# One set of 4 KB slots for all stages, and w_out's hi/lo parts kept in DRAM, in a retention and conv-FFN block

## The chip, the cores and the metric

The kernel runs on one core of a Trainium2 chip. The metric is the device time of one execution in microseconds (us). It is the median of several runs, and lower is better.

## The reference

One encoder layer on `x` of 2048 tokens by 1024 channels, in float32:

```python
proj = x @ w_in                                  # 1024 x 2560 -> q | k | v | g | p
ret  = retention(rope(q), rope(k) * 128**-0.5, v)   # 4 heads of 128, chunks of 64, state carried on
ret  = rmsnorm_head(ret) * silu(g)
pool = (trailing_mean(p, windows 2,4,8,16) - p) @ w_pool * pool_scale    # per group of 128
x = layernorm(alpha * x + concat(ret, pool) @ w_out)       # 1024 x 1024
val, gate = split(x @ w_up)                      # 1024 x 5632
x = layernorm(alpha * x + (silu(causal_conv3(gate)) * val) @ w_down)     # 2816 x 1024
```

## The kernel before, in words

**Arithmetic.** Each float32 operand of a large product is cut into a rounded part and its remainder (`split`, L87: a cast on ACT, L88, and a subtraction on DVE, L89). `mm3` (L91 to L94) makes a product from three matmuls: hi x hi, hi x lo, lo x hi. So an operand tile of 128 x 512 takes 4 KB of each partition for its two parts.

**Seven products for eight.** The three large multiplications work on 2 x 2 blocks by a seven-product scheme (`PRODUCTS`, L47): each pair of weight tiles (i) has seven products p1, p6, p2, p5, p7, p3, p4, whose left operands (`OPERANDS`: a11, s2, s1, a12, s3, a22, s4) are blocks of the activations or sums of blocks, and whose right ones (b.. and t..) are blocks of the weights or sums of them. One superblock is 1024 tokens; there are two. `class Seven` (L181) holds the operands of one superblock in seven tiles of 16 KB (a product each, four parts j), loads the weights four products ahead (`LOOK`, L53), makes the weights' sums in the first superblock and stores them to DRAM on POOL's queue (`w_sums`), and reads them back in the second (`again`, L249).

**Four stages.** `stage_in` (L518) makes q, k, v, p, g, in 10 pairs per superblock, and stores them to `proj`. The first pair is done in the plain way (`first_pair`, L259), with the sums of x made after it (`first_sums`, L206). During pairs 2 to 5 the sums of the second superblock are made and stored (`sums_to_dram`, L172), at pair 6 the first pair's weight sums, and at pairs 4 to 8 `fold` (L555) multiplies the pool group's matrix into the matching half of w_out and stores it to `w_pool_out`. In the second superblock the steps of retention and pooling (`Light`, L342) are laid between the products, 1.7 per product. `stage_mix` (L612) loads w_out (half of it from `w_pool_out`), splits it into `wo` tiles (L619 to L624), and for each of four blocks of 512 tokens multiplies (`contract`, L637), adds x, does the layer norm, and turns the rows (`turn`, L645: 8 transposes on PE, 2 copies on ACT, DMAs to `x1T` and `y1`). `stage_up` (L713) has 22 pairs per superblock, and makes and stores the gated, convolved activations and their sums (`to_down`, L750). `stage_down` (L810) multiplies by w_down and does the last norm.

**Memory.** Each stage opens pools of its own and closes them at its end; a later pool's tile that lies over an earlier one's waits for the last use of that tile. Shared by all stages are a ring of six 4 KB tiles for split weights (`new_w`, L146) and twelve 2 KB temporaries, five of them for loads of activations (`new_x`, L152) and seven for raw weights (`new_raw`, L153).

**Order.** The program is written as one stream; a scheduler at build time lays each engine's and each DMA queue's instructions out by its own estimate of when they are ready, the earlier in the program first among those that are. It may bring an instruction far forward. Instructions made through `behind` (L106) keep their order. At run time every queue goes in its order. Loads are issued on SP's queue, stores on POOL's.

## Time and profile before

| What | us |
|---|---|
| Median of 3 runs | 2059.79 (2059.72 to 2061.27) |
| The profiled execution, its own time | 2060.84 |
| Its span, first to last instruction | 2059.1 |
| TensorE busy in the span | 1960.2 |
| VectorE busy | 1418.5 |
| ScalarE busy | 807.4 |
| GpSimd busy | 406.8 |

The stages lie in the span at about 0 to 500 us (`stage_in`, its second superblock from 250), 500 to 755 (`stage_mix`), 755 to 1620 (`stage_up`, its second superblock from 1200) and 1620 to 2059 (`stage_down`). Where TensorE is fed, a product's matmuls start one after another; a stretch in which it was idle, or ran at the lower clock, shows as fewer matmuls than its length allows. The memory traffic over the whole span is 433.98 MB.

### The profile page before, as it was taken

The numbers are of one execution on the slowest core, as the hardware profiler recorded it, in microseconds if no ns is written. First come the engines' busy times: TensorE is split into PE (matmuls) and PEld (weight loads), VectorE is DVE, ScalarE is ACT, GpSimd is POOL, SyncE is SP. The second block draws the span as 40 slices with busy tenths as digits, with TensorE's granted clock in tenths as the row PEclk, the third lists the DMA queues.
The fourth block names the chain that finished last, engine by engine and source line by source line (L and its number), as shares of the span: only waits on it lengthen the run. The fifth ranks groups of instructions, "written<-read, shape, count | busy, mean of one in ns | idle before, by whom it ended". The sixth has DMA issues, their size and how long they took to land.

```text
span 2059.1 us, 26395 instructions
## 1 busy us (share of the span) xinstructions
PE 1960.2 (95%) x8849; PEld 1610.5 (78%) x8849; DVE 1418.5 (69%) x2167; ACT 807.4 (39%) x1314; POOL 406.8 (20%) x692
## 2 busy tenths in 40 slices
PE   7998899997899969989999999999999899999997
PEld 5777788886778847878888878888888688888886
DVE  6655687766675668778778786777766654455687
ACT  5334634433332235434444454444444443333321
POOL 1332112221132332233223211222211000000022
PEclk9999999999899989999999999999999999999999
DMA  8886788887777586575444574877744684444443
GB/s 270 281 270 238 231 245 233 242 266 247 232 229 226 205 276 218 184 235 192 157 158 170 169 258 131 280 252 242 268 144 154 224 312 143 140 136 128 156 166 124
DMA packets 195496, 433.98 MB, mean 211 GB/s; under 512 B 26272, under 2 KB 26272, under 8 KB 195360
## 3 DMA queue, kind: packets, MB, share of 16 engines
q1 hardware_dynamic: 148672, 278.64, 43.9%
q0 software_dynamic: 46112, 152.60, 20.3%
q8 instruction: 69, 1.13, 0.2%
q10 hardware_dynamic: 576, 1.05, 0.1%
q14 instruction: 67, 0.55, 0.1%
HBM read 277.53 MB, written 154.66 MB: 210 GB/s over the span
## 4 chain that ended last, share of the span: by engine, by line
PE 77%; DMA 8%; issue 7%; DVE 5%; POOL 2%; ACT 1%; SPq 0%; POOLq 0%; DVEq 0%; ACTq 0%
PE psz L94 9%; PE psz L92 9%; PE psz L93 9%; PE psy L93 7%; PE psy L92 7%; PE psy L94 7%; PE psw L92 6%; PE psw L93 6%; PE psw L94 6%; PE pl L104 3%; PE pl L93 2%; PE pl L94 2%; PE pl L92 2%; DMA mr<-mixT 1%; DMA xq<-in_xT 1%
## 5 line engine op out<-in xcount | busy, mean ns | idle before, releaser
L92 PE MATMUL psy<-opa,w 128*128 128x512 f32 x516 | 207.0, 401 | 16.0 <-ACT opa L88 12.2
L92 PE MATMUL psz<-ops,w 128*128 128x512 f32 x508 | 202.5, 399 | 9.2 <-ACT keptp L722 5.5
L93 PE MATMUL psy<-opa,w 128*128 128x512 f32 x516 | 205.1, 398 | 0.0
L94 PE MATMUL psy<-opa,w 128*128 128x512 f32 x516 | 204.2, 396 | 0.0
L94 PE MATMUL psw<-ops,w 128*128 128x512 f32 x504 | 198.1, 393 | 5.0 <-DVE w L89 5.0
L92 PE MATMUL psw<-ops,w 128*128 128x512 f32 x504 | 199.9, 397 | 1.8 <-ACT ops L88 0.9
L94 PE MATMUL psz<-ops,w 128*128 128x512 f32 x508 | 200.6, 395 | 0.0
L93 PE MATMUL psz<-ops,w 128*128 128x512 f32 x508 | 200.5, 395 | 0.1
L93 PE MATMUL psw<-ops,w 128*128 128x512 f32 x504 | 198.1, 393 | 0.7 <-DVE ops L89 0.7
L92 PEld LDWEIGHTS psy<-opa,w 128*128 128x128 f32 x516 | 99.3, 192 | 38.6 <-ACT opa L88 13.4
L92 PEld LDWEIGHTS psz<-ops,w 128*128 128x128 f32 x508 | 96.4, 190 | 32.9 <-ACT keptp L722 7.2
L313 POOL TENSOR_TENSOR rs<-mv,neg_half 128x1 f32<-128x1 f32 x32 | 38.4, 1200 | 410.4 <-DVE mv L329 410.1
L93 PEld LDWEIGHTS psy<-opa,w 128*128 128x128 f32 x516 | 99.0, 192 | 22.6 <-DVE opa L89 1.7
L94 PEld LDWEIGHTS psw<-ops,w 128*128 128x128 f32 x504 | 95.1, 189 | 26.0 <-DVE w L89 5.4
L94 PEld LDWEIGHTS psy<-opa,w 128*128 128x128 f32 x516 | 98.6, 191 | 21.3
L92 PEld LDWEIGHTS psw<-ops,w 128*128 128x128 f32 x504 | 95.3, 189 | 23.4 <-ACT ops L88 1.8
L94 PEld LDWEIGHTS psz<-ops,w 128*128 128x128 f32 x508 | 96.5, 190 | 21.0
L93 PEld LDWEIGHTS psz<-ops,w 128*128 128x128 f32 x508 | 96.3, 190 | 21.0 <-DVE ops L89 1.1
L93 PEld LDWEIGHTS psw<-ops,w 128*128 128x128 f32 x504 | 95.3, 189 | 21.1 <-DVE ops L89 1.2
L92 PE MATMUL psz<-opa,w 128*128 128x512 f32 x256 | 100.7, 393 | 0.0
L94 PE MATMUL psz<-opa,w 128*128 128x512 f32 x256 | 100.1, 391 | 0.0
L93 PE MATMUL psz<-opa,w 128*128 128x512 f32 x256 | 100.1, 391 | 0.0
(372 smaller groups left out, 4705.7 us busy)
## 6 DMA issues: line engine op xcount, KB each, us to landing
u_ops<-us POOLq DMA_DIRECT2D x88, 256.0 KB, 3.2
proj<-o POOLq DMA_DIRECT2D x80, 256.0 KB, 4.5
u_ops<-zz POOLq DMA_DIRECT2D x66, 256.0 KB, 2.6
again<-w_sums_in SPq DMA_DIRECT2D x40, 256.0 KB, 5.2
v<-in_w_up SPq DMA_DIRECT2D x35, 256.0 KB, 3.6
sg<-in_w_up SPq DMA_DIRECT2D x35, 256.0 KB, 2.7
old<-in_w_up SPq DMA_DIRECT2D x33, 256.0 KB, 2.6
z<-proj SPq DMA_DIRECT2D x64, 128.0 KB, 4.9
```

The source lines that it names most:

```text
L92: nc.tensor.matmul(ps, l_hi, r_hi, start=start, stop=False, **kw)
L93: nc.tensor.matmul(ps, l_hi, r_lo, start=False, stop=False, **kw)
L94: nc.tensor.matmul(ps, l_lo, r_hi, start=False, stop=stop, **kw)
L104: return lambda *a, **kw: tc.keep_in_program_order(f(*a, **kw))
L313: nc.gpsimd.tensor_tensor(dst, var, neg_half[:, :n], ALU.pow)
```

## The change

- The seven operand tiles of 16 KB become 28 named slots of 4 KB (`SLOTS`), in one pool that lives for the whole program. Each part j of an operand is a tile of its own.
- `stage_mix` takes its 16 `wo` tiles, its mixed operands (`u`, six in place of seven tiles), its rows y (5) and one norm vector from these slots; `stage_down` takes its 16 `wd` tiles and 12 of its 16 row tiles from them.
- All 16 tiles of w_out are split in the first superblock of `stage_in` and stored as hi and lo (512 KB each) to `w_out_parts`; of the 8 that belong to the pool half, the folded product is split from PSUM and stored. `stage_mix` loads them without a split. `w_pool_out` goes.
- The work beside the first superblock's products is laid out by a count of products (`clock`): from pair 2 on, every third product starts one of the four sums of x, then the first pair's weight sums; every second product starts the pool matrix, then one of the 16 parts of w_out. Their later steps follow 1 to 3 products on.
- `first_pair` loads each weight tile just before it is needed, and the second pair's weights are loaded ahead of `first_sums`.
- Light's steps in `stage_in` start some three products later. The sums of the first superblock for `stage_up` are made some 14 steps earlier, in the third block of `stage_mix` in place of the fourth.
- In `stage_up`, the tiles `kept` have 2 buffers in place of 1, `us` 2 in place of 4. `stage_in` and `stage_mix` use the pool `light` for their small tiles.

```diff
+SLOTS = {op: [op + str(j) for j in range(KH)] for op in OPERANDS}
+WO_SLOTS = SLOTS["a11"] + SLOTS["s2"] + SLOTS["s1"][2:] + SLOTS["s3"] + SLOTS["s4"][:2]
+U_SLOTS = SLOTS["a12"] + SLOTS["s1"][:2]
+Y_SLOTS = SLOTS["s4"][2:] + SLOTS["a22"][:3]
+GB_SLOT = SLOTS["a22"][3]
+WD_SLOTS = SLOTS["a11"] + SLOTS["s2"] + SLOTS["a12"] + SLOTS["s1"]
+ROW_SLOTS = SLOTS["s3"] + SLOTS["s4"] + SLOTS["a22"]
...
+    slots = ctx.enter_context(tc.tile_pool(name="slots", bufs=1))
...
         def split_op(self, sb, name, j, x):
-            if name not in self.ops[sb]:
-                slot = "s4" if name == "a21" else name
-                self.ops[sb][name] = self.op_pool.tile([P, 2, KH, TB], F32R, name="op" + slot)
-            o = self.ops[sb][name]
-            split(o[:, 0, j, :], o[:, 1, j, :], x)
+            slot = SLOTS["s4" if name == "a21" else name][j]
+            o = slots.tile([P, 2, TB], F32R, name=slot)
...
         def first_pair(self):
-            self.load_w(0)
...
                     if name not in w:
+                        self.load_w(0, names=(name,))
                         w[name] = self.prepare(-1, name)
...
                 self.first_pair()
+                self.load_w(1)
                 self.first_sums()
...
+            def later_sums(j):
+                return lambda: after(2, sums_to_dram(t["xT"], sums_in, 1, j))
+
+            def first_pair_sums():
+                st.load_w(0, new_x)
+                after(2, lambda: [st.sum_of_w(0, name) for name in ("t2", "t3", "t4")])
...
+                def keep(src):
+                    w = new_w()
+                    split(w[:, 0, :], w[:, 1, :], src)
+                    return w
+
+                def store(w):
+                    nc.gpsimd.dma_start(w_out_parts[n, j], w.bitcast(F32))
+
+                def fold(w):
+                    g, wpool, ps = OUT_ORDER[j] - H, kept["wpool"], aux_bank()
+                    mm3(ps, wpool[:, 0, cols(g)], wpool[:, 1, cols(g)], w[:, 0, :], w[:, 1, :],
+                        True, True)
+                    after(1, lambda: store(keep(ps)))
+
+                def load():
+                    raw = lp.tile([P, HALO + TB], F32, name="pw", bufs=2)[:, :TB]
+                    nc.sync.dma_start(raw, t["w_out"][n, j // 2, :, j % 2, :])
+                    if j // 2 in POOL_TILES:
+                        w = []
+                        after(2, lambda: w.append(keep(raw)))
+                        after(3, lambda: fold(w[0]))
+                    else:
+                        after(2, lambda: store(keep(raw)))
+                return load
...
+            begin = {3: [later_sums(j) for j in range(KH)] + [first_pair_sums],
+                     2: [pool_map] + [w_out_part(n, j) for n in range(2) for j in range(KD)]}
...
-                    due[0] += 1.7
+                    due[0] += 1.7 if (i, p) != (n, "p2") else -4.0
...
     def stage_mix(light):
+            new_wo, new_u, new_y = parts_in(WO_SLOTS), parts_in(U_SLOTS), rows_in(Y_SLOTS)
             for n in range(2):
-                for i in range(KD // 2):
-                    w = wo[n, i] = big.tile([P, 2, 1024], F32R, name="wo", bufs=8)
-                    src = w_pool_out if i in POOL_TILES else t["w_out"]
-                    for j in range(2):
-                        raw = wk.tile([P, 512], F32, name="raw2")
-                        nc.sync.dma_start(raw, src[n, i, :, j, :])
-                        split(w[:, 0, j * 512:(j + 1) * 512], w[:, 1, j * 512:(j + 1) * 512], raw)
+                for j in range(KD):
+                    wo[n, j] = new_wo()
+                    nc.sync.dma_start(wo[n, j].bitcast(F32), w_out_parts[n, j])
...
-                    if b == 3 and at[0] % 4 == 1 and at[0] < 16:
-                        sums_left.append(sums_to_dram(x1T, sums_up, 0, at[0] // 4))
-                    if at[0] % 4 == 0 and sums_left:
+                    now = 24 * b + at[0] - 58
+                    if now >= 0 and now % 4 == 0 and now < 16:
+                        sums_left.append(sums_to_dram(x1T, sums_up, 0, now // 4))
+                    if now % 4 == 3 and sums_left:
...
-                    kept[p] = wk.tile([P, TB], F32, name="kept" + p)
+                    kept[p] = wk.tile([P, TB], F32, name="kept" + p, bufs=2)
...
-                    r = wk.tile([P, TB], F32, name="us", bufs=4)
+                    r = wk.tile([P, TB], F32, name="us", bufs=2)
...
-                w = ws[p, f] = big.tile([P, 2, 512], F32R, name="wd", bufs=16)
+                w = ws[p, f] = new_wd()
...
-                    y = ys[sb, s, half] = big.tile([P, DM], F32, name="y4", bufs=4 * NS)
+                    y = ys[sb, s, half] = (new_row() if len(ys) < len(ROW_SLOTS) else
+                                           big.tile([P, DM], F32, name="y4", bufs=4))
```

## Rows read from the trace of the kernel before

**Rows 1.** The page: span, busy time and share of each engine.

```profile
span 2059.1 us, 26395 instructions
PE 1960.2 (95%) x8849; PEld 1610.5 (78%) x8849; DVE 1418.5 (69%) x2167; ACT 807.4 (39%) x1314; POOL 406.8 (20%) x692
```

**Rows 2.** Busy time by stretch: stretch, each engine's busy us (count), clock, DMA, GB/s.

```profile
36.00:66.00 30.00, 22.55 (x70) 16.11 (x69) 24.06 (x40) 15.38 (x28) 3.78 (x7) 0.77 0.88 281
66.00:152.00 86.00, 86.00 (x370) 69.08 (x369) 52.53 (x83) 32.78 (x58) 28.69 (x54) 1.00 0.83 275
152.00:166.00 14.00, 7.84 (x26) 5.73 (x25) 7.54 (x13) 4.83 (x9) 5.24 (x10) 0.76 0.92 304
166.00:250.00 84.00, 84.00 (x360) 66.99 (x359) 48.92 (x76) 45.71 (x84) 15.62 (x29) 1.00 0.67 223
250.00:263.00 13.00, 7.17 (x25) 5.54 (x25) 9.64 (x16) 6.30 (x12) 0.54 (x1) 0.74 0.84 247
...
499.00:545.00 46.00, 29.91 (x136) 24.49 (x135) 26.75 (x45) 17.32 (x29) 4.79 (x7) 0.78 0.81 264
545.00:612.00 67.00, 62.21 (x337) 51.00 (x336) 55.63 (x99) 19.29 (x32) 18.39 (x24) 1.00 0.71 212
...
735.00:765.00 30.00, 11.60 (x40) 8.43 (x38) 18.61 (x30) 11.12 (x19) 11.99 (x20) 0.66 0.88 301
765.00:790.00 25.00, 21.75 (x87) 15.45 (x88) 19.73 (x31) 17.71 (x31) 0.73 (x2) 1.00 0.86 271
...
890.00:924.00 34.00, 28.53 (x117) 22.79 (x117) 27.48 (x41) 11.88 (x19) 13.49 (x23) 0.95 0.65 220
924.00:1200.00 276.00, 276.00 (x1218) 228.31 (x1218) 211.87 (x298) 124.47 (x192) 71.18 (x131) 1.00 0.52 175
1200.00:1217.00 17.00, 13.06 (x50) 10.04 (x49) 15.98 (x24) 11.10 (x19) 2.94 (x6) 0.90 0.91 300
...
1610.00:1634.00 24.00, 16.25 (x62) 12.57 (x61) 16.62 (x24) 10.74 (x18) 3.21 (x6) 0.79 0.69 223
```

**Rows 3.** TensorE's waits, whole span: who waited for whom, us, times, longest.

```profile
PE pl L651 <- DVE y L335: 14.7, 2, 8.4
...
PE psy L92 <- ACT w L88: 11.6, 1, 11.6
PE pl L104 <- DMA vt<-proj: 5.8, 1, 5.8
PE psz L92 <- ACT keptp L722: 5.5, 2, 3.7
PE psw L94 <- DVE w L89: 5.0, 1, 5.0
...
PE psy L93 <- DVE wd L89: 4.1, 1, 4.1
```

**Rows 4.** Order of time, ScalarE, from the start: start, length, instruction, idle before.

```profile
3.43 0.62 ACT L88 CAST w<-v 128x512 fp32r<-128x512 f32 x1 [1.19 <-DMA v<-in_w_in]
6.61 0.62 ACT L88 CAST w<-sc 128x512 fp32r<-128x512 f32 x1 [2.56 <-DMA sc<-in_w_in]
...
8.25 0.62 ACT L88 CAST opa<-xq 128x512 fp32r<-128x512 f32 x1
```

**Rows 5.** Order of time: one VectorE instruction of the first superblock.

```profile
150.15 0.69 DVE L224 TENSOR_TENSOR qd<-vt,qd 128x512 f32<-128x512 f32 x1 [5.81 <-DMA proj<-o]
```

**Rows 6.** DMA issues: out<-in, queue, count, KB each, median us to landing.

```profile
u_ops<-us POOLq DMA_DIRECT2D x88, 256.0 KB, 3.2
...
w_pool_out<-o POOLq DMA_DIRECT2D x8, 256.0 KB, 5.0
```

**Rows 7.** Groups of VectorE between 499 and 545 us.

```profile
L89 DVE TENSOR_TENSOR wo<-raw,wo 128x512 fp32r<-128x512 f32 x14 | 9.4, 689 | 10.2 <-ACT wo L88 10.1
```

**Rows 8.** Order of time, VectorE, the last two of one group of sums.

```profile
976.48 0.68 DVE L759 TENSOR_TENSOR us<-us,zz 128x512 f32<-128x512 f32 x1
977.20 0.69 DVE L759 TENSOR_TENSOR us<-zz,us 128x512 f32<-128x512 f32 x1
```

More of the change, by code (lines that the diff above doesn't have):

```diff
@@ L144, in hybrid_block, with parts_in, rows_in @@
     tmp = ctx.enter_context(tc.tile_pool(name="tmp", bufs=1))
+    slots = ctx.enter_context(tc.tile_pool(name="slots", bufs=1))
+    def parts_in(names):
+        return rotating([lambda n=n: slots.tile([P, 2, TB], F32R, name=n) for n in names])
+    def rows_in(names):
+        return rotating([lambda n=n: slots.tile([P, DM], F32, name=n) for n in names])
     def new_w():
@@ L210, in first_sums, with load_w @@
                     self.split_op(0, name, j, a)
-        def load_w(self, i, new=new_raw):
-            r = self.raw[i] = {"new": new}
-            for n, name in enumerate(("b11", "b12", "b21", "b22")):
+        def load_w(self, i, new=new_raw, names=("b11", "b12", "b21", "b22")):
+            r = self.raw.setdefault(i, {})
+            r["new"] = new
+            for name in names:
                 r[name] = new()
-                nc.sync.dma_start(r[name], self.w_src[i, n])
+                nc.sync.dma_start(r[name], self.w_src[i, "b11 b12 b21 b22".split().index(name)])
         def sum_of_w(self, i, name):
@@ L305, in run @@
                     if i < 3:
-                        nc.tensor.matmul(z, w[:, 0, 0:P], x[:, 0, 0, :], start=True, stop=True,
+                        nc.tensor.matmul(z, w[:, 0, 0:P], x[0][:, 0, :], start=True, stop=True,
                                          skip_group_check=True)
@@ L518, in stage_in @@
     def stage_in(lp, light):
-        with ExitStack() as ph:
+        if True:
+            wk = lp
             kept = {}
@@ L562, in fold, with pool_map, finish @@
+            def first_pair_sums():
+                st.load_w(0, new_x)
+                after(2, lambda: [st.sum_of_w(0, name) for name in ("t2", "t3", "t4")])
+            def pool_map():
+                raw = lp.tile([P, HALO + TB], F32, name="pw", bufs=2)[:, :TB]
+                nc.sync.dma_start(raw, t["w_pool_t"])
+                scale = lp.tile([P, 4], F32, name="pscale")
+                nc.sync.dma_start(scale, t["pool_scale"])
+                def finish():
                     for g in range(4):
-                        nc.vector.tensor_scalar_mul(raw[:, cols(g)], raw[:, cols(g)], scale[:, g:g + 1])
+                        behind.vector.tensor_scalar_mul(raw[:, cols(g)], raw[:, cols(g)],
+                                                        scale[:, g:g + 1])
@@ L564, in fold @@
                     wpool = kept["wpool"] = lp.tile([P, 2, 4 * P], F32R, name="cs")
                     split(wpool[:, 0, :], wpool[:, 1, :], raw)
-                    return
-                (m, j), i = divmod(k // 2, 2), POOL_TILES[k % 2]
-                g, wpool = OUT_ORDER[2 * i + j] - H, kept["wpool"]
-                raw = lp.tile([P, HALO + TB], F32, name="pw", bufs=2)[:, :TB]
-                nc.sync.dma_start(raw, t["w_out"][m, i, :, j, :])
-                w = new_w()
-                split(w[:, 0, :], w[:, 1, :], raw)
@@ L573, in fold, with w_out_part @@
[L573 to L578 removed]
+                after(2, finish)
+            def w_out_part(n, j):
+                def keep(src):
[10 more added lines that the diff above has]
+                def load():
+                    raw = lp.tile([P, HALO + TB], F32, name="pw", bufs=2)[:, :TB]
+                    nc.sync.dma_start(raw, t["w_out"][n, j // 2, :, j % 2, :])
[6 more added lines that the diff above has]
+                return load
@@ L580, in ready, with after @@
+            def after(steps, f):
+                todo.append((clock[0] + steps, f))
+            begin = {3: [later_sums(j) for j in range(KH)] + [first_pair_sums],
+                     2: [pool_map] + [w_out_part(n, j) for n in range(2) for j in range(KD)]}
+            todo, clock = [], [0]
             def ready(b, h):
                 return b < 2 or here[0] >= n + 4 + 2 * h
-            here, due, sums_left = [0], [0.0], []
+            here, due = [0], [0.0]
             def hook(i, p):
@@ L589, in hook @@
                     light.constants()
-                if p == "p1" and 2 <= i < 6:
-                    sums_left.append(sums_to_dram(t["xT"], sums_in, 1, i - 2))
-                if p == "p7" and sums_left:
-                    sums_left.pop()()
-                if i == 6 and p == "p1":
-                    st.load_w(0, new_x)
-                    for name in ("t2", "t3", "t4"):
-                        st.sum_of_w(0, name)
-                if p == "p2" and 4 <= i < 9:
-                    for k in ((-1,), (0, 1), (2, 3), (4, 5), (6, 7))[i - 4]:
-                        fold(k)
+                if 2 <= i < n:
+                    clock[0] += 1
+                    for item in [x for x in todo if x[0] <= clock[0]]:
+                        todo.remove(item)
+                        item[1]()
+                    for period, works in begin.items():
+                        if works and clock[0] % period == 0:
+                            works.pop(0)()
                 if i == n - 1 and p == "p1":
@@ L633, in load_mix @@
                 else:
-                    m = mix[b, k] = big.tile([P, 2, TB], F32R, name="u", bufs=7)
+                    m = mix[b, k] = new_u()
                 split(m[:, 0, :], m[:, 1, :], raw)
```

63 lines of the change are left out of this document (27 added, 36 removed).

## The prediction, made before the changed kernel was run

> **What bounds the kernel now.** I read the page first: TensorE is busy for 1960 us of 2059 and, its own weight loads aside, no other engine for over 1420 [rows 1]. So almost the whole time is matmuls that the change doesn't touch, and the question is which of TensorE's holes it closes and which it opens. The second view is the busy time by stretch, cut where the matmul count drops [rows 2]. From 924 to 1200 us TensorE is fed: 276 us for 1218 matmuls, 0.227 us each. At that pace the holes are: 36 to 66 us, 30 - 70 x 0.227 = 14.1; 152 to 166, 8.1; 765 to 790, 5.3; 890 to 924, 7.4; 1200 to 1217, 5.6; 1610 to 1634, 9.9. Where small matmuls mix in I take idle time alone, a lower bound since the clock is low after a hole: 250 to 263, 5.8; 499 to 545, 16.1; 545 to 612, 4.8; 735 to 765, 18.4. With the start, where the first operand is split only at 8.25 us [rows 4], that is about 104 us, and it is all that a better order could win. The stretches 66 to 152 and 166 to 250 lose only 2.2 and 2.3 us [rows 2]. The third view, TensorE's waits [rows 3], says what each hole is: the turns of the last rows wait for the layer norm (14.7 us, two waits), the first product of the second stage for its first split operand (11.6), retention's first transposes for a load (5.8), stage three for a copy that needs a buffer (5.5), stage four for splits (4.1 the longest listed).
>
> **The change part by part.** Gains are positive; each has its bounds in brackets.
>
> Start. The weights b11, b21, b12, b22 go ahead of x on SP's queue. The first tile is split at 3.43 us, the third loaded at 6.61, the fifth (x) at 8.25 [rows 4]. With x in second place it would be there about half way between 3.43 and 6.61, at 5.0, so 3.2 us sooner; but the same 20 loads follow at the same pace, and part is lost again. I take 2 (0 to 4).
>
> 36 to 66 us. VectorE is busy for 24 of 30 us there and the loads for 0.88 of the time [rows 2]. The second pair's weights come sooner, but the second superblock's sums come denser. I take 0 (-6 to 8).
>
> The fold's stall (152 to 166). VectorE stood 5.81 us before a weight sum of the first pair [rows 5] (the row puts it down to a store; the sum reads two loads issued just before), with the fold's splits behind it and TensorE behind those. The sums now follow their loads by two products, the fold its split by one. I take 8 (0 to 8).
>
> The denser first superblock. This is the cost. Per pair there are 4 weight loads, 4 sums stored and 4 outputs stored, 12 x 0.262 = 3.15 MB. The plan's 17 items at every second product take 34 products, and with their tails 35 products, five pairs: 15.7 MB. Beside them: four sums of x, 32 x 0.262 = 8.4 MB; 16 parts of w_out, 0.262 in and 0.524 out, 12.6 MB; the pool matrix 0.3 and the first pair's sums 2.1. Together 39.1 MB, of which the new traffic is 8.4 (8 more loads, 2.1 MB; stores 8.4 for 2.1). A product takes 12 matmuls in 86 / 370 = 0.232 us each, 2.79 us [rows 2], so 35 take 98 us, and that asks for 400 GB/s. In 66 to 152 the engines moved 275 GB/s at 0.83 busy, so 331 when full [rows 2]. The 39.1 MB then need 118 us, 20 us over. Some of it may slip into 166 to 250, where the DMA engines are idle for a third. Splits add 24 - 8 = 16 on VectorE of 0.69 us, 11 us, and 16 casts of 0.62 less 8 copies on ScalarE; VectorE is busy for 61% and 58% there and hides them, while the loads come; if they don't, everything behind a waiting split stands. SP's queue gets 8 more issues, POOL's 8 more; a store stands behind whichever split it waits for, and the outputs' stores behind it. I take half of the overrun, -10 (-25 to 0). The Trainium skill ("DMA: Bandwidth & Descriptors", Specifications) gives some 358 GB/s per core as the limit; by that, as an estimate, the plan would run 11 us over and this term would be near -5. No stretch of [rows 2] reached it; the densest, 304 GB/s at 0.92, is full at 330.
>
> Retention starts later (250 to 263). Its loads no longer compete with the operands', so the 5.8 us wait [rows 3] mostly goes: 5 (0 to 5.8). Some six of its steps move into the next stage, where TensorE does the same work.
>
> Start of the second stage (499 to 545). Now 16 tiles are loaded, split and queued before and between the mixed operands, 14 of them inside this stretch: 9.4 us of VectorE [rows 7] and as many casts. In the changed kernel the tiles a11 and s2 are free after the first and second but one products of the last pair, so 8 ready tiles arrive some 10 us before the end, and the mixed operands have VectorE to themselves. What is late next is the mixed operand's load, behind the norm vector's load on SP if the latter waits for the last slot a22. I take 13 of 16.1 (8 to 16). The 16 splits were VectorE's in 545 to 612 too in part: 1 (-4 to 4.8).
>
> End of the second stage (735 to 790), 18.4 + 5.3. Before, the third stage's operand pool could lie over the rows y and wait for the last turn. Now a11 and s2 are free once the first column half of the last block is done, four times 8 steps (some 22 us) before the end, and their sums are made a block earlier. Two products, 24 x 0.227 = 5.4 us, can run in the norm's wait, the third needs a12, which is freed at the last step. The turns still sit somewhere in TensorE's order, and a22 waits for the rows to be stored. I take 11 (3 to 20).
>
> 890 to 924. The copy of `kept` waited for its one buffer [rows 3]; two give slack: 3 (-5 to 7.4), with the sums that block VectorE unchanged.
>
> Two `us` tiles. The fourth sum starts 0.72 us after the third [rows 8] and now waits for the store of the second before it, 3.2 us after its issue [rows 6]: some 2 us of VectorE in each of 22 groups. It has 23% idle [rows 2], and only its weight splits would pass this on: -1 (-5 to 0).
>
> 1200 to 1217: the operands are freed part by part, but the loads, 0.91 busy, stay: 0 (-4 to 5). Start of the fourth stage (1610 to 1634): `wd` lies in slots that are free three products earlier; the splits are still queued on VectorE behind the last sums: 5 (0 to 9.9). The first-stage sums' earlier place, the rows' slots and the end cost nothing: the matmuls of 612 to 735 and 1634 on cover them; uncovered, they would be a split or a load each, about a microsecond.
>
> Sum: 2 + 0 + 8 - 10 + 5 + 13 + 1 + 11 + 3 - 1 + 0 + 5 = 37 us. The profiled execution took 2060.84 (span 2059.1); 2060.8 - 37 = 2023.8. The median stands 1.05 below that execution: 2022.8, say 2023.
>
> **The rivals.**
>
> Slots held by stores (slower). The hi and lo of a part lie in the ring of six tiles that feeds the products until their 512 KB store has landed. A 256 KB store of the fold took 5.0 us [rows 6]; one of 512 KB between 5 and 10. With cast, subtraction and issue (0.62 + 0.69 + 0.54) a tile is held 7 to 12 us, while products want four of the six. If TensorE waits for half of 7 us in each of 16 parts, 56 us are lost; the other terms are 47, so 2060.8 - 47 + 56 - 1 = 2069. It decides from 47 / 16 = 2.9 us per part. For it: DMA is 0.83 busy there already. Against: 66 to 152 loses nothing now, with the fold's tiles in the same ring, and ready products come before parts. 13%. The Trainium skill (the same page, Anatomy of one DMA) puts a transfer at 2.0 us plus its bytes at 436 GB/s; as an estimate 3.2 us for such a store, and the rival would fall away. The 5.0 us above for half the bytes stands against it.
>
> The stage ends stay closed. SP and VectorE go in their order, and the three stage changes give only their lower bounds, 8 + 3 + 0 for 29: 2023 + 18 = 2041. For it: each of those holes has a load, a split and the norm in a row. 17%.
>
> Everything is covered: no overrun (+10) and the three changes near their upper ends (+11): 2002. For it: the idle third of the DMA engines in 166 to 250. 16%.
>
> It doesn't do what it says: the scheduler pulls the spread work forward as the old order did, the loads pile up in 36 to 166, and the overrun and new stalls eat the gains: 2060, no change. 7%.
>
> **How the numbers follow.** The forecast gets 47%, its own range 2010 to 2035. This kernel's runs can tell about 0.2%, 4 us, from no change. Faster: 47 + 17 + 16 = 80%; same 7%; slower 13%. The range takes the forecast, the stage ends that stay closed, the covered case but for its edge and the unchanged one: 1995 to 2060; outside lie the slower rival and a little below. The bounds of all terms, -38 to 89, reach further, but don't fall on one side together.
>
> **What would show it.** Right: no hole over 3 us before the first `wo` matmul; stage three's first product before the last turns; no wait for `kept` near 900; none for `vt` near 258; first matmul near 6 us. Wrong: holes between 66 and 250 us, where there were two small losses, with waits for w from ACT or DVE, and the DMA share there near 0.95; or the 11.6 and 14.7 us waits still in the list.

## The result, and the profile after

The changed kernel is slower: 2074.35 us (median of 15 runs, 2064.8 to 2081.64) beside 2061.27 for the kernel before in the same session (15 runs), a ratio of 1.0059 with a 95% interval of 1.0044 to 1.0074, so about 12 us. The forecast was 37 us the other way, and the time lies outside its range. The profiled execution is the one of 2081.64 us, the slowest of the 15 and 7 us above their median, so losses counted in it come out larger than the medians' 12 us.

The page of the changed kernel: span, busy times and traffic, to hold against [rows 1].

```profile
span 2079.8 us, 26413 instructions
PE 1965.2 (94%) x8849; PEld 1617.8 (78%) x8849; DVE 1410.0 (68%) x2167; ACT 800.5 (38%) x1306; POOL 414.6 (20%) x700
...
DMA packets 198313, 446.57 MB, mean 215 GB/s; under 512 B 26528, under 2 KB 26528, under 8 KB 198176
```

The same matmuls, a little less of VectorE and ScalarE, and 12.6 MB more traffic than the 433.98 MB before: 8.4 MB in the first superblock, and 4.2 MB where the second stage loads 16 ready parts of 512 KB in place of 16 raw tiles of 256 KB.

Busy time by stretch in the changed kernel, the stretches of [rows 2]; the columns are stretch, PE, PEld, DVE, ACT, POOL (counts), clock, DMA share, GB/s.

```profile
36.00:66.00 30.00, 18.39 (x59) 12.89 (x59) 20.84 (x34) 11.20 (x20) 3.23 (x6) 0.81 0.80 269
66.00:152.00 86.00, 72.95 (x289) 57.95 (x288) 46.98 (x77) 27.40 (x50) 27.37 (x52) 0.91 0.85 295
152.00:166.00 14.00, 10.07 (x35) 7.83 (x36) 8.02 (x13) 6.82 (x13) 3.84 (x9) 0.76 0.96 342
166.00:250.00 84.00, 79.23 (x340) 64.57 (x339) 46.60 (x72) 37.92 (x69) 19.85 (x37) 0.98 0.68 231
250.00:263.00 13.00, 13.00 (x60) 10.74 (x59) 9.64 (x16) 10.17 (x19) 1.08 (x2) 1.00 0.79 260
499.00:545.00 46.00, 42.32 (x229) 35.76 (x227) 26.33 (x48) 11.59 (x20) 9.49 (x15) 1.00 1.00 329
545.00:612.00 67.00, 55.29 (x277) 46.03 (x278) 45.01 (x81) 13.80 (x23) 8.03 (x11) 0.87 0.78 236
...
890.00:924.00 34.00, 33.56 (x148) 27.47 (x147) 26.58 (x38) 13.94 (x21) 9.87 (x19) 1.00 0.67 231
924.00:1200.00 276.00, 271.97 (x1191) 224.14 (x1190) 210.28 (x297) 114.71 (x174) 81.04 (x146) 0.99 0.52 175
1200.00:1217.00 17.00, 17.00 (x77) 14.08 (x76) 14.84 (x22) 12.39 (x20) 1.03 (x2) 1.00 0.78 251
1610.00:1634.00 24.00, 24.00 (x108) 19.88 (x107) 15.75 (x23) 11.16 (x18) 3.17 (x6) 1.00 0.56 183
```

From 66 to 152 us TensorE started 370 matmuls before and 289 now. The holes of 250 to 263 and of 1610 to 1634 are gone. But the work has shifted against the clock, by some 20 us from 160 us on, so a hole can be missing here and stand a little further on. Finer cuts of the same kernel show where the holes now are:

```profile
60.00:80.00 20.00, 18.64 (x66) 14.13 (x67) 13.27 (x24) 9.29 (x17) 3.46 (x7) 0.80 0.54 176
...
100.00:120.00 20.00, 14.51 (x52) 10.87 (x51) 10.25 (x16) 6.48 (x13) 5.91 (x11) 0.83 0.87 301
120.00:140.00 20.00, 14.21 (x51) 11.17 (x50) 8.77 (x15) 6.26 (x12) 4.84 (x9) 0.83 0.91 327
140.00:160.00 20.00, 14.31 (x55) 11.04 (x54) 10.81 (x18) 5.50 (x11) 6.96 (x13) 0.83 0.95 349
...
520.00:540.00 20.00, 20.00 (x111) 17.14 (x110) 10.01 (x19) 4.17 (x7) 4.06 (x7) 1.00 1.05 353
540.00:560.00 20.00, 8.73 (x31) 6.59 (x30) 3.37 (x5) 3.46 (x6) 0.00 (x0) 0.74 0.87 301
```

Three stretches from 100 to 160 us give some 52 matmuls each where 88 fit, while DMA goes from 0.87 to 0.95 busy. Just before, at 60 to 80, DMA is at 0.54; that dip goes with the new start and not with the dense work (0.60 in run E3 below, which has the new start without the dense work, 0.72 in E13, which has the dense work without the new start). At 540 TensorE stops again.

To compare kernels whose work is shifted, I laid each trace's matmuls in order and counted each at the pace it has when TensorE is fed (0.2266 us for 512 columns, 0.111 for 128). The start of a matmul less the sum of those before it is the time lost so far. By stretches of that work, in us lost:

```
                       before   after   change
first matmul               8.9     5.3    +3.6
work 0 to 40              17.6    23.2    -5.6
40 to 200 (1st superbl.)  13.3    33.3   -20.0
200 to 440 (2nd superbl.) 13.9    24.5   -10.6
440 to 500 (stage 2 start)24.6    21.5    +3.1
500 to 640 (stage 2)       5.5    17.2   -11.7
640 to 700 (stage 2 end)  28.5    14.4   +14.1
700 to 1480 (stage 3)     14.2    13.5    +0.7
1480 to 1520 (stage 4)    10.5     4.5    +6.0
all                      137.2   157.4   -20.2
```

The last line is the difference of the two profiled executions (2081.64 - 2060.84 = 20.8) within a microsecond. "Loss" below means this count. It is read from one execution of each kernel, and that one can stand some us off its kernel's median (E6's is 7 us below); a stretch that an edit doesn't touch moves too (200 to 440 us of work has 17 to 28 us in the runs that keep the parts and the later retention). So a difference of a few us in one stretch shows little, and what a kernel gains as a whole is told by the ratios.

TensorE's waits in the changed kernel, whole span (who waited for whom, us, times, longest), to hold against [rows 3]:

```profile
PE psy L100 <- ACT w L96: 11.3, 1, 11.3
PE psw L100 <- ACT s L96: 9.7, 2, 4.9
PE pl L100 <- ACT w L96: 9.6, 3, 4.2
PE pl L112 <- DVE old L112: 9.5, 5, 3.1
PE pl L693 <- DVE a L350: 8.5, 3, 6.0
PE pl L101 <- DVE w L97: 7.8, 4, 5.8
PE psz L100 <- ACT keptp L765: 7.5, 5, 2.8
PE psw L100 <- DVE a L709: 7.5, 1, 7.5
```

The 11.6 us wait of the second stage's first product is gone; one of 11.3 stands two operands further on, as the next lines show. The turns' 14.7 is down to 8.5. New are the waits for the fold's splits (`pl`, L100 and L101) and for retention's state (`old`).

**The second stage's start** in the changed kernel. SP's queue in order of time (start, length, instruction), before and in the hole:

```profile
513.11 0.86 SPq L672 DMA_DIRECT2D again<-mixT  x2
...
523.85 11.11 SPq L664 DMA_DIRECT2D s<-w_out_parts  x11
542.80 0.32 SPq L449 DMA_DIRECT2D sg<-proj  x1
543.21 0.38 SPq L664 DMA_DIRECT2D s<-w_out_parts  x1
543.68 0.38 SPq L667 DMA_DIRECT2D a<-in_ln_g  x1
544.16 1.67 SPq L672 DMA_DIRECT2D again<-mixT  x3
```

ScalarE there:

```profile
551.92 0.62 ACT L96 CAST w<-again 128x512 fp32r<-128x512 f32 x1 [18.70 <-DMA again<-mixT]
```

The first two mixed operands are issued at 513.11, and TensorE starts the stage with them at 532.43, without a hole. The third stands behind eleven loads of 512 KB and a load of retention's that is issued at 542.80, though the eleven had been issued by 534.96. Who held SP's queue between 500 and 560 us (waited for, us, times, longest):

```profile
SPq L449 <- DMA mixT<-sg: 8.9, 2, 7.8
```

That load needs the buffer of a store that is still on its way, and holds all behind it for 7.8 us. So the third operand is issued only at 544.16, split at 551.92, and TensorE goes on at 552.59. Bytes and a wait of the queue are both in this hole.

### The profile page after: what moved, and what is told of

Same layout as the page of the kernel before. It is cut to its first block, busy times and chain, and to the rows that moved or that the text cites. A ratio compares the mean times of both kernels' runs of the same rounds, so it can differ in the third digit from the quotient of the medians.

```text
span 2079.8 us, 26413 instructions
## 1 busy us (share of the span) xinstructions
PE 1965.2 (94%) x8849; PEld 1617.8 (78%) x8849; DVE 1410.0 (68%) x2167; ACT 800.5 (38%) x1306; POOL 414.6 (20%) x700
## 4 chain that ended last, share of the span: by engine, by line
PE 63%; DMA 14%; issue 9%; DVE 8%; POOL 3%; ACT 2%; SPq 0%; POOLq 0%; DVEq 0%; ACTq 0%
PE psz L100 8%; PE psz L102 8%; PE psz L101 8%; PE psy L100 6%; PE psy L101 6%; PE psy L102 6%; PE psw L101 5%; PE psw L100 5%; PE psw L102 5%; PE pl L101 2%; PE pl L102 2%; PE pl L100 2%; DMA again<-mixT 1%; DMA s<-w_out_parts 1%; PE pl L112 1%
## 5 line engine op out<-in xcount | busy, mean ns | idle before, releaser
L100 PE MATMUL psy<-a,w 128*128 128x512 f32 x614 | 245.8, 400 | 21.4 <-ACT w L96 11.3
L100 PE MATMUL psz<-s,w 128*128 128x512 f32 x600 | 239.0, 398 | 11.2 <-ACT keptp L765 7.5
L101 PE MATMUL psy<-a,w 128*128 128x512 f32 x614 | 243.7, 397 | 0.0
L100 PE MATMUL psw<-s,w 128*128 128x512 f32 x550 | 219.6, 399 | 25.1 <-ACT s L96 9.7
L102 PE MATMUL psy<-a,w 128*128 128x512 f32 x614 | 242.6, 395 | 0.0
L101 PE MATMUL psz<-s,w 128*128 128x512 f32 x600 | 236.2, 394 | 0.2 <-DVE s L97 0.2
L102 PE MATMUL psz<-s,w 128*128 128x512 f32 x600 | 236.1, 394 | 0.0
L101 PE MATMUL psw<-s,w 128*128 128x512 f32 x550 | 217.0, 395 | 0.6 <-DVE s L97 0.6
L102 PE MATMUL psw<-s,w 128*128 128x512 f32 x550 | 216.4, 393 | 0.0
L100 PEld LDWEIGHTS psy<-a,w 128*128 128x128 f32 x614 | 118.1, 192 | 47.5 <-ACT w L96 11.7
L100 PEld LDWEIGHTS psz<-s,w 128*128 128x128 f32 x600 | 114.3, 191 | 38.5 <-ACT keptp L765 9.8
L100 PEld LDWEIGHTS psw<-s,w 128*128 128x128 f32 x550 | 105.0, 191 | 50.3 <-ACT s L96 10.7
L100 PE MATMUL psz<-a,w 128*128 128x512 f32 x357 | 141.7, 397 | 1.2 <-DVE g L771 1.0
L101 PE MATMUL psz<-a,w 128*128 128x512 f32 x357 | 140.2, 393 | 0.0
L102 PE MATMUL psz<-a,w 128*128 128x512 f32 x357 | 140.0, 392 | 0.0
L101 PEld LDWEIGHTS psy<-a,w 128*128 128x128 f32 x614 | 117.8, 192 | 25.7 <-DVE a L97 1.4
L102 PEld LDWEIGHTS psy<-a,w 128*128 128x128 f32 x614 | 117.9, 192 | 24.8
L102 PEld LDWEIGHTS psz<-s,w 128*128 128x128 f32 x600 | 114.1, 190 | 24.5 <-DVE w L97 0.3
L101 PEld LDWEIGHTS psz<-s,w 128*128 128x128 f32 x600 | 114.3, 191 | 23.7 <-DVE s L97 0.5
L101 PEld LDWEIGHTS psw<-s,w 128*128 128x128 f32 x550 | 104.9, 191 | 22.9 <-DVE s L97 1.7
L102 PEld LDWEIGHTS psw<-s,w 128*128 128x128 f32 x550 | 104.8, 191 | 22.0
```

Source lines behind the costliest of these rows:

```text
L100: nc.tensor.matmul(ps, l_hi, r_hi, start=start, stop=False, **kw)
L101: nc.tensor.matmul(ps, l_hi, r_lo, start=False, stop=False, **kw)
L102: nc.tensor.matmul(ps, l_lo, r_hi, start=False, stop=stop, **kw)
```

## The experiments

Ratios are to the kernel before, run on the same chip beside each; all have a 95% interval. The changed kernel's own is 1.0059.

**E1, stores that hold no ring tile.** The rival that I had priced at 2069 us.

```diff
-                    nc.gpsimd.dma_start(w_out_parts[n, j], w.bitcast(F32))
+                    nc.gpsimd.dma_start(w_out_parts[n, j], kept["wpool"].bitcast(F32))
```

> The 512 KB stores of the first superblock read one resident tile (the pool matrix's hi and lo) in place of the ring tile just split; bytes, issues and their order stay, and the wrong data in w_out_parts is left so. Theory A, ring slots held by stores: in the changed kernel ScalarE waits 46 us (12 waits) for landings of w_out_parts between 60 and 260 us; these go, the first superblock wins back 15 us or more of the 22 it lost, 2052 to 2060 us. Theory B, too many bytes: the loads stay late, little changes, 2068 to 2077. Theory C, VectorE behind sums whose loads are late: same as B in time, with waits of VectorE for x.

Measured: 1.0059 (1.0042 to 1.0076), loss in the first superblock 30.4 for 33.3. In the changed kernel ScalarE's waits between 60 and 260 us had begun with the stores:

```profile
ACT w L96 <- DMA w_out_parts<-w: 46.4, 12, 7.7
```

In E1 they begin with VectorE:

```profile
ACT w L96 <- DVE w L97: 43.0, 12, 14.2
```

And VectorE's own in E1, in the same stretch, have loads at their head once the splits' own casts are set aside:

```profile
DVE sq L239 <- DMA old<-in_w_in: 13.5, 1, 13.5
DVE xq L112 <- DMA xq<-in_xT: 9.2, 1, 9.2
```

The 46 us of waiting for stores go, and 43 us of waiting for something else stand in their place. So tiles held by stores are not what the stretch loses by; late loads fit the waits that are left. The rival's time was near, its mechanism falls.

**E2, the same work spread out; E10, half of that.** E2 starts the parts at every third product and the sums at every seventh; E10 changes the first line alone.

```diff
-            begin = {3: [later_sums(j) for j in range(KH)] + [first_pair_sums],
-                     2: [pool_map] + [w_out_part(n, j) for n in range(2) for j in range(KD)]}
+            begin = {7: [later_sums(j) for j in range(KH)] + [first_pair_sums],
+                     3: [pool_map] + [w_out_part(n, j) for n in range(2) for j in range(KD)]}
```

> The parts of w_out start at every third product in place of every second, the sums of x at every seventh in place of every third; nothing else. B (bytes): 39 MB go over some 50 products, 140 us, 280 GB/s, under what the engines can do, so most of the 22 us come back, 2050 to 2058. A (holds): each of the 16 parts still holds its ring tile until it lands, with landings somewhat shorter; a part comes back, 2062 to 2070. C: the denser sums are what blocks VectorE; about as B.

> Only the sums of x start at every seventh product; the parts of w_out stay at every second. Theory C, that the dense sums are what holds the queues: 25 or less lost between 40 and 200 us of work, 2064 to 2068. Theory B, bytes: only 6 of 39 MB move later, 29 to 33 stay lost, 2071 to 2076.

Measured: E2 1.002 (1.0009 to 1.0031), first superblock 23.6; E10 1.0041 (1.0023 to 1.0059), 27.5. Spreading wins back 0.39%, 8 us, clear of the noise; the sums alone about half by the median, which the intervals don't settle.

**E5, no bytes; E9, no bytes and spread.** 15 of 16 stores write 32 columns of 512 in each half, and the second stage loads the one whole part 16 times, so the bytes of its loads stay; E9 has E2's lines too.

```diff
+                    c = TB if n == j == 0 else 32
-                    nc.gpsimd.dma_start(w_out_parts[n, j], w.bitcast(F32))
+                    nc.gpsimd.dma_start(w_out_parts[n, j][:, :, 0:c], w[:, :, 0:c].bitcast(F32))
...
-                    nc.sync.dma_start(wo[n, j].bitcast(F32), w_out_parts[n, j])
+                    nc.sync.dma_start(wo[n, j].bitcast(F32), w_out_parts[0, 0])
```

> Of the 16 stores of hi and lo, the first stays whole and 15 carry 32 of 512 columns of each half (32 KB); the second stage loads the first part 16 times, so all bytes of its loads stay and the data is wrong. All splits, issues and places of the program are the changed kernel's; 7.4 MB go from the first superblock. Theory B, bytes: of the 33 us lost there between 40 and 200 us of work, the 18 come back that the slots alone gave back: 15 to 20 lost, 2054 to 2060. Theory C, the new order (the sums every third product, VectorE and ScalarE standing before late loads): 25 or more stay lost, 2066 to 2074.

> Small stores (as in the fifth run, data wrong in the same way) and the wide spread (as in the second) together. Between 40 and 200 us of work: changed kernel 33 lost, wide spread 23, small stores 22, slots alone 15. If bytes and density are one cause (DMA full), both together give what either gives, some 20 to 22. If they are two, bytes for the engines and density for the queues' order, they add to 13 to 16, as before.

Measured: first superblock 22.4 and 21.6; ratios 1.0051 (1.0031 to 1.007) and 1.0003 (0.9987 to 1.002). In the count of that stretch, taking the bytes away and spreading the work win the same 10 us, and both together no more, as one cause would. The times don't bear this out: E5 can't be told from the change (1.0059), while spreading wins 8 us with the bytes (E2) and 10 without them (E9 beside E5). So that the work is too dense there is shown; that it is the stores' bytes is not. Some 8 us over the kernel before stay with neither bytes nor density.

**E3, the slots alone.** The first superblock's order and w_out's loads and splits are those of before; all else is the change.

```diff
-            begin = {3: [later_sums(j) for j in range(KH)] + [first_pair_sums],
...
+                if p == "p2" and 4 <= i < 9:
+                    for k in ((-1,), (0, 1), (2, 3), (4, 5), (6, 7))[i - 4]:
+                        fold(k)
...
-                    nc.sync.dma_start(wo[n, j].bitcast(F32), w_out_parts[n, j])
+                    raw = wk.tile([P, TB], F32, name="again", bufs=3)
...
+                    split(wo[n, j][:, 0, :], wo[n, j][:, 1, :], raw)
```

> The first superblock's fold, its sums and their places are those of the kernel before, and the second stage loads and splits w_out as before; slots, first pair, later start of retention, earlier sums for stage three and the buffer numbers are the changed kernel's. A and B both: the first superblock's 22 us come back, the 9 won at the second stage's start go; the ends of stages two and three keep their 14 and 6: 2061 to 2069. If the slots themselves cost time in the first superblock, it stays at 2074 or above.

Measured: 1.0027 (1.0011 to 1.0042). First superblock 15.4, stage two's end 13.3, stage four's start 1.1: the slots and the earlier sums together are worth what was hoped. But 26.7 is lost in the second superblock and 32.1 at stage two's start, where raw tiles and mixed operands share three buffers.

**E4, the mixed operands ahead; E11, half of w_out later; E12, the same and spread.** Three tries to clear the way for the mixed operand that is late.

```diff
 E4
+                    if n == 0:
+                        load_mix(0, OUT_ORDER[j])
 E11, E12 (in the first block's steps)
+                    if b == 0:
+                        load_wo(1, j)
```

> At the start of the second stage the loads of the eight mixed operands stand between the first eight of w_out, in place of behind all sixteen. Theory D, loads in the wrong order on SP's queue: the hole of 11.4 us at 552 us closes to under 4, 2064 to 2069. Rival, DMA is simply full there (353 GB/s in 520 to 540): the hole stays at 8 or more, 2072 to 2076.

> The second eight parts of w_out are loaded one by one in the first block of the second stage, and the mixed operands' loads stand between the first eight. Theory G, the start of the second stage is bound by 8.4 MB of w_out where it was 4.2, at 353 GB/s: the 21.5 us lost between 440 and 500 us of work fall to 8 to 12, 2060 to 2066. Rival, retention's own loads and stores hold the queue: 18 or more stay, 2070 to 2076.

> The wide spread and the late second half of w_out together. If the gains add, 2065 less 8 to 12: 2053 to 2057, faster than the kernel before. If one moves the other's hole, 2062 to 2066.

Measured: 1.0057 (1.0038 to 1.0076), 1.0086 (1.0062 to 1.011), 1.0027 (1.0014 to 1.004); loss at stage two's start 22.7, 24.9 and 23.3 beside 21.5. The 11.3 us wait is gone in all three, and the loss stays: TensorE now waits for retention's loads and steps, which share the queue. From 480 to 575 us, its longest wait in E11:

```profile
PE pl L112 <- DMA vt<-proj: 7.2, 1, 7.2
```

So E11's rival held and its theory failed: with half of w_out's bytes out of the way the start loses as much.

**E6, retention at its old place; E7, stage three's sums at theirs; E8, both, and spread.**

```diff
 E6
-                    due[0] += 1.7 if (i, p) != (n, "p2") else -4.0
+                    due[0] += 1.7
 E7
-                    now = 24 * b + at[0] - 58
+                    now = 24 * b + at[0] - 73
```

> Retention's steps in the first stage start at once again, 1.7 per product. The changed kernel lost 24.5 us between 200 and 440 us of work where before lost 13.9. Theory E, the later start moves retention's steps into a place where the products' loads and the next stage's loads meet them: 6 to 10 come back, 2064 to 2068. Rival, the ten were lost to loads of the next stage and to chance: nothing comes back, and the wait for the first load at the start returns: 2074 to 2080.

> The first superblock's sums for stage three are made in the fourth block again (first at its step 1, every fourth step). Theory F, made early they block VectorE for 10 us on turned rows not yet in DRAM, and TensorE waits 7.6 us at 757 us: that hole goes, 10 come back in the second stage and 3 to 5 are lost at its end: 2066 to 2070. Rival, the hole moves to the later place: 2073 to 2078.

> The wider spread of the second experiment with both of the last two. If the gains add: 2065 less 6 to 8 for retention and 6 to 8 for the sums, 2049 to 2054, faster than the kernel before. If retention's and the sums' losses were the scheduler's chance, 2062 to 2068.

Measured: E6 1.0094 (1.0077 to 1.0111): by the count 9 us back in the second superblock (15.2) and 9 in stage two (8.6), 11 lost at its start (32.5); in time it is slower all the same, and its profiled execution is the fastest of its four, so the count flatters it. E7 1.0095 (1.008 to 1.011): 10 back in stage two (7.1), 13.5 lost at its end (27.9). So the early sums, not the slots by themselves, close the hole at that end, and by the count they cost 10 us before it. E8 1.0055 (1.0039 to 1.0071): the losses move as in its parts (37.7 at stage two's start, 0.9 in it), and beside E2 0.35% is lost, 7 us. E6 and E7 too are each 0.35% behind the change, clear of the noise: with the parts in place, the later retention and the earlier sums are each worth some 7 us.

**E13, the old start; E14, the old start and spread.**

```diff
         def first_pair(self):
+            self.load_w(0)
...
-                        self.load_w(0, names=(name,))
...
-                self.load_w(1)
```

> The change but for its start: the first pair's four weight tiles are loaded ahead of x again, and the second pair's after the first sums. Theory (the new order of the start is what loses: TensorE starts 3.6 us sooner, but its first matmuls then wait one by one for b21, b12 and b22, which come behind four x tiles each): the first 40 us of work lose about 18 us in place of 23, and the time is some 5 us below the change, near 2068. Rival (the loss there is that of 20 loads at one pace, whatever their order): the first 40 us of work stay near 23, the first matmul goes back to 8.9 us, and the time is that of the change, 2074, or a little above.

> The parts of w_out at every third and the sums at every seventh product, and the old start. Theory (the two losses are apart and add): 10 us below the change by the spreading, 5 by the start, so near 2060, the time of the kernel before. Rival (the start's loss only moves into the sums that follow): near 2066, as with the spreading alone, with more lost between 40 and 200 us of work than the 23.6 there.

Measured: 1.0047 (1.0031 to 1.0062) and 1.0008 (0.9995 to 1.0021). The loss from 0 to 40 goes to 17.1 and 16.6, as said, but the first matmul goes back to 9.7 and 8.9; I had left that out of the price. Both together, the new start costs 1.7 us in the first pair of runs (28.5 - 26.8) and 2.6 in the second (28.1 - 25.5), but the intervals of both pairs overlap.

**E15 and E16, slots without the parts; E17, with them.** E15 is E3 with the old start and w_out's raw tiles in the four buffers `o`; E16 is E15 with retention at its old place; E17 is E14 with retention at its old place.

```diff
 E15, E16 (against E3)
-                    raw = wk.tile([P, TB], F32, name="again", bufs=3)
+                    raw = wk.tile([P, TB], F32, name="o", bufs=4)
 E16, E17
-                    due[0] += 1.7 if (i, p) != (n, "p2") else -4.0
+                    due[0] += 1.7
```

> The slots, the earlier sums and the later retention, but the first superblock as before with the old start, and w_out split in the second stage as before, its raw tiles in the four buffers o in place of the three that it shared with the mixed operands in the run with the slots alone. Theory (in that run w_out's raw tiles and the mixed operands held each other up in three shared buffers, which made its loss at the second stage's start 32 us where the kernel before has 25): 25 us or less there, 18 in the first 40 us of work, and a time near 2067 - 7 - 6 = 2054, below the kernel before. Rival (the loss at the stage's start is that of SP's one queue, not of buffers): still near 32 there, and a time near 2061.

> The same with retention's steps in the first stage as early as in the kernel before. Theory (retention's place only moves the loss between its own stretch and the second stage's start, as in the run of the change with early retention): 10 us less lost between 200 and 440 us of work, 10 more at the second stage's start, and the same time as the run beside it within 4 us. Rival (with buffers of their own w_out's tiles no longer collide with retention's last steps): 14 us lost between 200 and 440 as before, the stage's start no worse than the run beside it, and a time near 2044.

> The change with w_out's parts at every third product, the sums at every seventh, the old start, and retention as early as in the kernel before. It differs from the run with slots, own raw buffers, old start and early retention by the hi and lo parts alone, kept in DRAM or not. Theory (what makes the second stage's start late with early retention is the load of the ready parts, 512 KB each, on SP's queue ahead of and between the mixed operands and retention's loads): 8 to 10 us less lost between 200 and 440 us of work than with the late retention (22), 10 or more lost again at the stage's start (30 and more), and a time near 2061. Rival (the parts' loads are harmless, and the old start and the spreading were all that was missing): 14 us lost between 200 and 440, near 22 at the stage's start, and a time near 2050.

Measured, medians, ratios with intervals, and loss in four stretches of work:

```
     w_out's parts   retention  median   ratio (interval)           40-200 200-440 440-500 500-640
E14  kept in DRAM    later      2061.9   1.0008 (0.9995 to 1.0021)    21.3    22.4    20.6    15.9
E17  kept in DRAM    as before  2066.0   1.0025 (1.0013 to 1.0037)    20.5    20.8    34.5     8.7
E15  split in stage2 later      2058.0   0.9993 (0.998 to 1.0007)      9.7    28.9    26.3    14.7
E16  split in stage2 as before  2039.0   0.9898 (0.9876 to 0.992)      9.7    12.2    25.4     9.7
```

E16 beats both kernels, by 1.0% (21 us) the one before. So the theory of E16 failed and its rival held; E15 lies between its two. E14 and E15 differ by the parts, and so do E17 and E16 (with them goes the first superblock's order: by products with the parts, that of before without). With the parts, retention's later place is worth 0.17%, some 4 us, with intervals that overlap (with the dense work, E6 beside the change, 0.35%, clear of them); without the parts it costs 19. And at retention's old place the parts cost 1.27% of 2060, 26 us; by the count, 11 in the first superblock, 9 in the second, 9 at stage two's start. At its later place they cost 0.15%, which the intervals don't tell from nothing. So what either costs depends on the other. The 9 in the second superblock were not foreseen (E17's text says 8 to 10 less than with the late retention, and 1.6 less came); no run says what they are. What E17 waits for at the stage's start, TensorE's waits from 440 to 560 us:

```profile
PE psy L100 <- ACT w L96: 24.8, 1, 24.8
```

E17, SP's queue in order of time:

```profile
517.35 11.48 SPq L663 DMA_DIRECT2D s<-w_out_parts  x9
529.79 0.33 SPq L666 DMA_DIRECT2D a<-in_ln_g  x1
531.08 2.88 SPq L671 DMA_DIRECT2D again<-mixT  x3
```

E16, SP's queue:

```profile
473.99 7.19 SPq L644 DMA_DIRECT2D again<-mixT  x3
...
501.01 7.24 SPq L635 DMA_DIRECT2D o<-w_pool_out  x2
```

E16 issues its first mixed operands at 474 us and w_out at 501; E17 has them the other way round, the operands at 531, behind the ready parts. So the parts change the order as well as the bytes, and these two runs don't tell one from the other. TensorE's waits there in E16:

```profile
PE psy L100 <- ACT a L96: 5.6, 1, 5.6
PE psz L100 <- DVE o L542: 4.3, 1, 4.3
PE pl L112 <- DVE old L112: 3.3, 1, 3.3
```

One wait of 24.8 us against several of 3 to 6. Behind the second superblock's start E15 waits for retention's state, E16 hardly at all. TensorE's waits from 255 to 480 us, in E15:

```profile
PE pl L112 <- DVE old L112: 7.2, 4, 3.6
PE pl L112 <- DVE xk L112: 3.7, 1, 3.7
PE pl L112 <- DMA vt<-proj: 0.8, 1, 0.8
```

and in E16:

```profile
PE pl L112 <- DVE sg L112: 0.3, 1, 0.3
```

Just before that stretch E16 has the first wait for `vt`, which the later start was to remove:

```profile
PE pl L112 <- DMA vt<-proj: 6.6, 1, 6.6
```

In E15 it is gone but for 0.8, and more than it is lost behind it.

## Why the prediction was wrong

Right was where the time would go, what would be won at the ends, and that the first superblock is "the cost". Wrong were four terms of the sum, all of them places where work was added or moved and I took the cover for granted, and priced each as if the others were not there. Term by term, forecast and count (the count stands some 8 us higher in all than the medians):

- **The denser first superblock, with the fold's stall: -10 + 8, measured -20.** The failed term. The sign, the traffic (8.4 MB) and the view that shows it (0.95 busy, waits for w) were as written. The step that failed is the price of the overrun, bytes over a full rate of 331 GB/s, half of it lost. That rate is too low: 392 was reached (below), at which the plan's 39.1 MB take 100 us beside the products' 98, so by bytes alone almost nothing would be lost, and 20 us are. The "idle third of the DMA engines in 166 to 250" is still there (0.68) and did not take it up. What the runs show in its place: the density costs 8 us (E2), tiles held by stores are not it (E1), and that it is bytes is not shown (E5). Another 6 stay when the stores' bytes and the density are gone (E9 21.6 beside E3 15.4, both with the new start); whether they are the order by products or the 16 parts' splits stays open. In E1 VectorE stands up to 13.5 us before one load, with the splits of its queue behind it, but no run takes such waits out. The fold's +8 was not won either: its matmuls wait for the same splits in smaller pieces, 9.6 + 7.8 us in the list. The Trainium skill ("DMA: Bandwidth & Descriptors", Specifications) gives some 358 GB/s per core as the limit; the trace does not agree, it passes that by a tenth over 20 us (392), and the measurement decides.
- **Start of the second stage: +13, measured +3.** I took out 16 splits and left the queue as it was. The bytes on it doubled, 16 x 0.524 = 8.4 MB where 4.2 stood, at 353 GB/s 24 us in place of 12, and they stand in front of the third mixed operand; a load of retention's holds the queue for 7.8 us more. The sentence on what is late next named the mixed operand's load and gave it no price. The sign "no hole over 3 us before the first `wo` matmul" came true, and the hole came two operands later. How much is bytes and how much order stays open: E17 beside E16 loses 9 us more here with the parts (34.5 against 25.4), E14 beside E15 loses 6 less (20.6 against 26.3), and half of the bytes moved away wins nothing (E11).
- **Retention later: +5, measured -10.6 in the second superblock.** It does what the term says (0.9 us of waiting for `vt` where 5.8 were). Without the parts it costs far more than it wins, E15 beside E16: 19 us of time, by the count 16.7 in that stretch and 5 from 500 to 640. "Where TensorE does the same work" was the false part. With the parts in place the times say the reverse: at its old place the kernel is 7 us slower (E6), or 4 and not clear of the noise (E17 beside E14). So as a part of this change its price came out near, by luck and not by the way I gave; the second stage's start loses 11 to 14 us more at the old place (E6, E17), and why the two depend on each other is not shown.
- **545 to 612, and the sums' earlier place at nothing: +1, measured -11.7 from 500 to 640 us of work.** "Uncovered, they would be a split or a load each" was wrong by ten: E7 gets 10 us back there by moving the sums. In the changed kernel VectorE stands in one place 10.45 us for a load of `x1T`, with the norm's additions behind it, for which TensorE waits 7.5 us:

```profile
752.75 0.69 DVE L112 TENSOR_TENSOR vt<-qd,vt 128x512 f32<-128x512 f32 x1 [10.45 <-DMA vt<-x1T]
```

- **End of the second stage: +11, measured +14.1.** Right, by the step named (the sums a block earlier): E7 gives 13.5 of it back.
- **The start: +2, measured -2.0** (+3.6 for the first matmul, -5.6 behind it); E13 and E14 say -1.7 and -2.6, within the noise. In size it matters little.
- **`kept`, `us` and 1200 to 1217: +2, measured +0.7.** 890 to 924 lost 7.4 and now 34 - 148 x 0.2266 = 0.5; but 924 to 1200 lost nothing and now 276 - 1191 x 0.2266 = 6.1, for the longest wait for `kept` has moved with the work, from 917 us (3.7) to 942 (2.8). It isn't gone, as I had said it would be; all such waits are 7.5 us in five where they were 5.5 in two.
- **Start of the fourth stage: +5, measured +6.0.** Right in size; no run takes this part out by itself.

The rival "stage ends stay closed" describes one of the two ends. The slower rival came near in time, by luck: it had its decision in tiles held by stores, which E1 rules out. The Trainium skill (the same page, Anatomy of one DMA) would have dropped that rival by an estimate of 3.2 us for a 512 KB store; the trace has these stores at 5.3 us in the median, so the measurement decides against the figure, though not for the rival. DMA issues of the changed kernel, with twelve of the loads that bring the parts back:

```profile
w_out_parts<-w POOLq DMA_DIRECT2D x16, 512.0 KB, 5.3
...
s<-w_out_parts SPq DMA_DIRECT2D x12, 512.0 KB, 11.9
```

## What to carry to other kernels

Work that is prepared earlier and kept in memory must be priced at both ends: in the queues and engines where it is made and stored, and where it comes back at twice the size in front of an operand that the next stage waits for. Against 9.4 us of VectorE that had been saved [rows 7], the parts cost 26 us here with retention at its old place. And a change that bundles several parts is read by its cells: retention's place was worth some +4 or -19 us depending on the parts, so neither could be judged with the other left in. The best cell, slots without the parts and retention as before (E16), is 21 us faster than the kernel before.

## What was not expected of the hardware

The DMA engines moved 353 GB/s from 520 to 540 us, and more while TensorE stood in the hole behind it, where I had worked out 331 as a full rate from the kernel before:

```profile
530.00:550.00 20.00, 11.32 (x58) 9.09 (x56) 5.45 (x10) 2.33 (x4) 2.98 (x5) 0.90 1.03 392
```

E17 has 390 from 520 to 540, and the kernel before itself 371 at a share of 0.99 from 1638 to 1658. So GB/s divided by the share at 0.83 did not give the rate at 1. At that rate a 512 KB load took 11.9 us in the median from issue to landing, and a queue's load behind eleven of them comes late however early the first is issued. In E4 and E11, which put the operands between, that wait is gone and retention's loads wait in its place.
